# Decoder trunk on one core: the scheduler plans table loads and first landings, the key blocks get column parts of their own, the last products stand behind the gates, and the order is new

## The chip, the core and the metric

The kernel runs on one core of one Trainium2 chip: TensorE (PE) multiplies, VectorE (DVE), ScalarE (ACT) and GpSimd (POOL) do the elementwise work, SyncE (SP) issues the DMAs, and 16 DMA engines carry them. The metric is device microseconds of one execution. A measurement here is a median of three runs.

## The reference

Two layers of a decoder trunk over 256 tokens of width 1024, in float32. Per layer, cut to what matters:

```python
proj = rmsnorm(h, norm_g[i]) @ w_in[i]          # 14 groups of columns
# HGRN2: a gated linear recurrence over 4 heads (q, forget gate f, input, two output gates)
log_f = logaddexp(log(lb), log1p(-lb) + log_sigmoid(fl)); k_hg = (1 - lb) * sigmoid(-fl)
o_hg = hgrn2_chunkwise(q, log_f, k_hg, v)
y_hg = rmsnorm(o_hg) * sigmoid(hgo) * silu(hz)
# NSA: 8 heads, three branches over keys: compressed blocks, selected blocks, window
p_cmp = masked_softmax(q_nope @ kc.T * scale); o_cmp = p_cmp @ vc
o_nsa = gates[0]*o_cmp + gates[1]*selected_attn(q_rope, ...) + gates[2]*window_attn(q_rope, ...)
h = h + concat([y_hg, o_nsa * silu(nz)]) @ w_out[i]
gate = sigmoid(rmsnorm(h, ple_norm_g[i]) @ w_pg[i])
h = h + gate * (p[i] @ w_pp[i])
```

## The kernel before

**Products in three passes.** Every large product splits both operands in a rounded part and a rest (`xh`, `xl` and `hi`, `lo`, in the fp32r format) and sums three matmuls of 128 rows by 256 columns. A chunk of 256 weight columns (1 MB) is 48 such matmuls in one PSUM bank. There are three banks for this (`mm_63`, `mm_64`, `mm_65`), four for all else (`ax`), and one for the attention output (`po`). The `w_in` columns make 17 chunks (`hi0` to `nz1`; the chunk `kk` has 280 columns and takes two banks), and after them come `w_pp`, four chunks of `w_out` and four of `w_pg`.

**Loads and splits.** `loader` issues all weight DMAs from SP, in the order of the list `ORDER`, into four 1 MB buffers (`raw`). `splitter` makes `hi` (L505, on ACT or POOL) and `split_lo` makes `lo` (L511 on DVE, L512 on POOL) of a quarter chunk at a time, in a ring of nine buffers (`hl`). The weights `w1` of the compression go through the same `raw` buffers and hold two of them until their product (L986).

**What follows a chunk.** The chunks `hf` give the gates F and K (ACT Sigmoid), `hi` gives the values `tV` (L740, scaled by a factor that the row norm delivers), `hq` the queries. `tree` builds the decayed products of the recurrence: `near` for steps inside 32 tokens (L776), `blocks(32)` and `blocks(64)` for the larger ones (L835, evacuated by ACT, L839), then a last scaling of `tQ` and `tK` (L396 on DVE, L397 on POOL) and the product of `hgrn` (L888). `cmp_softmax` runs beside it: an Exp on ACT (L1291), a mask, sums. `attention` makes eight units per layer of scores, Exp, transposes and products (L1384 to L1442, L1360). `pp` multiplies p by `w_pp` (L1553) and keeps the result; `ev_pg` takes a `w_pg` bank, scales it (L1623), makes the gate with a Tanh, multiplies by the kept product and adds to h. The last `w_pg` chunk goes out in two halves (`ev_tail`, `tail_part`, L1662 to L1669).

**What sets the order.** `Sched.run` plays all of this at build time as threads of operations on planned clocks of five engines. At each step it takes the operation with the smallest planned start plus a weight (`WGT`) times a priority (`PRI`); some operations may go to one of two or three engines by a bias (`PREF`). The order it finds is the program's order on each engine. Its costs are plain numbers (`dS`, `dV`, `dG`); a change of ScalarE's function table has none. One table load stands at the start (L385); the others stand where a function first needs one:

```python
    S.activation(warm, ones, AF.Sigmoid)
    for _ in range(7):
        PE.matmul(sch.pools["ax"][-1].ap, lhsT=zb, rhs=zb[:, None, :].to_broadcast([128, 4, 128]),
```

Each engine takes its instructions strictly in this order, so an operation that waits holds all that stand behind it.

## Time and profile before

| | us |
|---|---|
| median of 3 runs (lowest to highest) | 392.29 (390.48 to 392.95) |
| the profiled execution, its own time | 392.22 |
| its span, first to last instruction | 390.4 |
| PE busy in the span | 379.2 |
| DVE, ACT, POOL busy | 309.3, 263.4, 126.2 |

A start time in a row counts from the start of the span. "Idle before" names the engine's idle time ahead of an instruction and what ended it. A busy time of PE is the time in which at least one matmul was in flight; matmuls overlap, so the pace is read from one start to the next. PEclk is the granted TensorE clock: 1.00 is the level of 2.4 GHz and 0.50 that of 1.2 GHz.

### The profile page before, as it was taken

What the parts mean: (1) busy time and instruction counts of PE and PEld (TensorE: products, weight loads), DVE (VectorE), ACT (ScalarE), POOL (GpSimd) and SP (SyncE); (2) the same over time, 40 slices, a digit from 0 to 9 for tenths busy, and PEclk for the clock granted to TensorE, in tenths of its full rate; (3) what the DMA queues carried; (4) which work ended last, traced back from release to release, by engine and by line L of the source; (5) the groups of instructions that cost most, each with busy time, mean ns of one, the idle gap of its engine ahead of it and who ended that gap; (6) DMA issues with size and microseconds to landing.
All of it is one profiled execution on the core that took longest, in us unless ns stands there. A gap on an engine that the chain in (4) does not pass through costs nothing.

```text
span 390.4 us, 9546 instructions
## 1 busy us (share of the span) xinstructions
PE 379.2 (97%) x3681; PEld 365.3 (94%) x3681; DVE 309.3 (79%) x731; ACT 263.4 (67%) x611; POOL 126.2 (32%) x195
## 2 busy tenths in 40 slices
PE   8989999999999999999999999999989999999995
PEld 4979999999899999999998999999989999999994
DVE  4984789999779875598978769999978787748864
ACT  6964455467788987486765945645878897857621
POOL 3000554556237544000000035724733755400100
PEclk9999999999999999999999999999999999999999
DMA  7995556454224431346446355935434342233011
GB/s 250 405 421 203 187 219 250 138 190 166 97 90 156 169 109 49 133 146 217 164 170 215 121 206 163 375 112 175 152 107 138 109 169 68 91 109 107 2 54 55
DMA packets 12285, 63.02 MB, mean 161 GB/s; under 512 B 1616, under 2 KB 2768, under 8 KB 5584
## 3 DMA queue, kind: packets, MB, share of 16 engines
q1 hardware_dynamic: 12240, 62.42, 44.5%
q8 instruction: 29, 0.48, 0.5%
q14 instruction: 16, 0.13, 0.1%
HBM read 61.36 MB, written 1.05 MB: 160 GB/s over the span
## 4 chain that ended last, share of the span: by engine, by line
PE 84%; DVE 6%; ACT 3%; DMA 3%; issue 1%; SPq 1%; DVEq 0%; ACTq 0%
PE mm L549 65%; DMA raw<-w_in 3%; PE po L1360 3%; PE mm L1553 3%; PE ax L1435 3%; DVE lo L511 2%; PE ax L776 2%; PE ax L1384 1%; ACT hi L505 1%; PE ax L1385 1%; PE ax L986 1%; SPq L400 1%; PE ax L1127 1%; PE po L1346 1%; ACT L1291 1%
## 5 line engine op out<-in xcount | busy, mean ns | idle before, releaser
L505 ACT ACTIVATE hi<-raw 128x512 fp32r<-128x512 f32 (+2 forms) x209 | 129.5, 628 | 83.0 <-PE mm L549 71.9
L549 PE MATMUL mm<-xh,hi 128*128 128x256 f32 x608 | 176.4, 290 | 1.8 <-ACT tV L740 1.8
L511 DVE TENSOR_TENSOR lo<-raw,hi 128x512 fp32r<-128x512 f32 (+2 forms) x201 | 142.1, 718 | 38.5 <-ACT hi L505 33.0
L549 PE MATMUL mm<-xl,hi 128*128 128x256 f32 x608 | 171.5, 282 | 0.0
L549 PE MATMUL mm<-xh,lo 128*128 128x256 f32 x608 | 171.1, 281 | 0.0
L549 PEld LDWEIGHTS mm<-xh,hi 128*128 128x128 f32 x608 | 115.1, 189 | 4.3 <-ACT tV L740 2.0
L549 PEld LDWEIGHTS mm<-xh,lo 128*128 128x128 f32 x608 | 115.7, 190 | 0.2 <-DVE lo L511 0.2
L549 PEld LDWEIGHTS mm<-xl,hi 128*128 128x128 f32 x608 | 115.4, 190 | 0.3
L549 PE MATMUL mm<-hi,xh 128*128 128x256 f32 (+1 forms) x192 | 55.5, 289 | 1.0 <-DVE t L1623 0.8
L549 PE MATMUL mm<-lo,xh 128*128 128x256 f32 (+1 forms) x192 | 54.5, 284 | 0.6 <-DVE lo L511 0.5
L549 PE MATMUL mm<-hi,xl 128*128 128x256 f32 (+1 forms) x192 | 54.1, 282 | 0.0
L1418 POOL TENSOR_SCALAR P<-P,s 128x128 f32<-128x128 f32 (+1 forms) x64 | 41.9, 673 | 30.4 <-DVE s L1411 12.3
L549 PEld LDWEIGHTS mm<-hi,xh 128*128 128x128 f32 x192 | 36.1, 188 | 2.6 <-ACT hi L505 1.4
L549 PEld LDWEIGHTS mm<-lo,xh 128*128 128x128 f32 x192 | 36.1, 188 | 1.2 <-DVE lo L511 1.2
L598 POOL TENSOR_TENSOR s<-s,mhalf 128x2 f32<-128x2 f32 x4 | 3.4, 846 | 104.1 <-DVE s L594 104.1
L549 PEld LDWEIGHTS mm<-hi,xl 128*128 128x128 f32 x192 | 36.2, 188 | 0.0
L1398 ACT ACTIVATE P<-P,s 128x128 f32<-128x128 f32 (+1 forms) x64 | 28.3, 447 | 0.0
L1393 DVE CUSTOM_DVE_ANT_0 P<-ax,cn 128x128 f32<-128x128 f32 (+1 forms) x64 | 20.3, 352 | 7.3 <-PE ax L1385 4.6
L1191 POOL TENSOR_TENSOR s<-s,mhalf 128x4 f32<-128x4 f32 x4 | 4.6, 1151 | 42.2 <-DVE s L1187 42.2
L397 POOL TENSOR_TENSOR md<-t,rp 128x32 f32<-128x32 f32 (+1 forms) x32 | 14.7, 479 | 6.3 <-DVE t L1111 4.0
L1442 ACT ACTIVATE PT<-ax 128x512 f32<-128x512 f32 x24 | 14.2, 592 | 3.1 <-PE ax L1435 3.1
L1435 PE MATMUL ax<-cn,P 128*128 128x128 f32 x96 | 14.5, 273 | 0.0
(210 smaller groups left out, 579.5 us busy)
## 6 DMA issues: line engine op xcount, KB each, us to landing
raw<-w_in SPq DMA_DIRECT2D x28, 1024.0 KB, 5.0
raw<-w_out SPq DMA_DIRECT2D x8, 1024.0 KB, 4.9
raw<-w_pg SPq DMA_DIRECT2D x8, 1024.0 KB, 4.8
raw<-w SPq DMA_DIRECT2D x4, 1024.0 KB, 5.0
...
raw<-w_pp SPq DMA_DIRECT2D x2, 1024.0 KB, 4.8
...
```

Source lines behind the costliest of these rows:

```text
L397: ("G", dG2(n), lambda: G.tensor_tensor(out, in0, in1, op=fn), PREF["t2_G"])], r, w)
L505: ("S", dS(m), lambda: S.activation(hi, src, AF.Copy), 0.0)], rt, ht_)
L511: yield alt([("V", dV2(m), lambda: V.tensor_tensor(lo, src, hv, op=OP.subtract), 0.0), ("G", dG2(m), lambda: G.tensor_tensor(lo, src, hv, ...
L549: PE.matmul(out, lhsT=a, rhs=b, start=k == 0 and i == 0 and (j == 0 or nb == 2), stop=k == NK - 1 and i == 2, skip_group_check=True)
L776: PE.matmul(pa[r0:r0 + 32, g], lhsT=Kx[:, hd, b:b + 32], rhs=qx[:, :, hd, b:b + 32], start=True, stop=True)
L1360: PE.matmul(po.ap[64 * par:64 * par + 64, tt * 128:(tt + 1) * 128], lhsT=vn[:, st, b, par], rhs=PTs[tt][par][b * (tt + 1) + st], start=Fal ...
L1393: yield op("V", dV(ns) + 0.02, lambda: V.tensor_tensor_reduce(P[:, b], sv[:, b], cn[:, CN_CA + 128 - ns + 128:CN_CA + 256], -1.0, 3.0e38, ...
L1398: yield op("S", dS(ns, 2), lambda: S.activation(P[:, b], P[:, b], AF.Exp, bias=nm.ap[:, b:b + 1], scale=-1.0, accum_out=sm_.ap[:, b:b + 1] ...
L1418: ("G", dG(ns) + 0.05, lambda: G.tensor_scalar(P[:, b], P[:, b], w, 1.0, op0=OP.mult, op1=OP.mult), PREF["P_G"]),
L1435: PE.transpose(tb.ap[:, i * 128:(i + 1) * 128], Ps[par][1][:, b, st * 128:(st + 1) * 128], idf)
L1442: ("S", dS(w_), lambda: S.activation(PT.ap[:, 0:w_], tb.ap[:, 0:w_], AF.Copy), PREF["PT_S"])],
L1553: PE.matmul(bk.ap[:, j * 256:(j + 1) * 256], lhsT=x[:, k, w], rhs=y[:, t], start=k == 0 and i == 0, stop=k == 1 and i == 2)
```

## The change

- **Order searched anew.** `ORDER` starts with `hf0, hi1, hi0` and ends with `nz0`; all planner tables (`WGT`, `PREF`, `MARG`, `STAY`, `PRI`) have new numbers. The compression weights `w1` are loaded after the fifth chunk and no longer after the ninth.
- **Table loads are planned.** An ACT operation may name its table; a change of table costs the planner 1.28, and a new thread issues a one-element Exp once all Sigmoids of a layer are done, and a one-element Sigmoid once the attention of the first layer is.
- **First landings.** The first two pieces of the first chunk are issued from ACT's queue, the first table load stands behind them, and the planner counts 1.0 and 0.6 more for two landings of h. The first two chunks may take their `hi` on DVE.
- **Column parts.** In `blocks`, key blocks of the two token halves write different partitions of PSUM, so that neighbouring matmuls use different columns of the array: two parts of 64, or four of 32. Each half gets its own evacuation on ACT. The compressed keys are repeated to 120 columns.
- **Last products.** p is halved when it is split. In the last layer the fourth `w_pp` chunk is multiplied after the last `w_pg` matmul; the gates are made meanwhile, and the sum reads the product from PSUM. The halves of 128 tokens are gone.

```diff
-ORDER = ["hi0", "hf0", "hi1", "hq0", "kk", "cm", "hf1", "hq1", "nq0", "hgo0", "nq1", "vv", "hz0", "nz0", "hz1",
-         "hgo1", "nz1"]
+ORDER = ["hf0", "hi1", "hi0", "hq0", "kk", "cm", "hf1", "hq1", "nq0", "hgo0", "nq1", "vv", "hz0", "hz1", "nz1",
+         "hgo1", "nz0"]
-BUFS = dict(mm=3, ax=4, raw=4, w1=8, t5=3, P=4, PT=5, t2=2, au=3, hl=9, wt=9)
+BUFS = dict(mm=3, ax=4, raw=4, w1=4, t5=3, P=4, PT=5, t2=2, au=3, hl=9, wt=9)
...
+            if isinstance(dur, Act) and dur.table != self.table:
+                end, self.table = end + 1.28, dur.table
+                self.eng[eng] = end
...
-    S.activation(warm, ones, AF.Sigmoid)
...
+        if act:
+            return op("S", Load(0.43, kb), lambda: nc.scalar.dma_start(out=out, in_=src), w=w)
...
-        pa, pb = pieces(items[0], (1, 1, 2, 2, 2)), pieces(items[1], (2, 2, 2, 2))
+        pa, pb = pieces(items[0], (1, 1, 2, 2, 2), 2), pieces(items[1], (2, 2, 2, 2))
         yield from next(pa)
+        yield from next(pa)
+        yield op("S", 1.49, lambda: S.activation(warm, ones, AF.Sigmoid))
...
+                if key in (items[0][0], items[1][0]):
+                    ch.append(("V", dVf(m), lambda: V.tensor_copy(hi, src), PREF["hi_V"]))
...
-                pa = bk.ap.rearrange("p (g t) -> p g t", g=8)
+                pa = bk.ap[:, 0:4 * lv].rearrange("p (h t) -> p h t", h=4)
+                bs = [(b % 128 // (2 * lv) * 2 * lv + b // 128 * lv, b) for b in range(0, T, 2 * lv)]
...
-                        for b in range(0, T, 2 * lv):
-                            r0 = b % 128
-                            PE.matmul(pa[r0:r0 + lv, 2 * hd + b // 128, 0:lv], lhsT=K[:, hd, b:b + lv],
+                        for r0, b in bs:
+                            PE.matmul(pa[r0:r0 + lv, hd], lhsT=K[:, hd, b:b + lv],
                                       rhs=Q[:, hd, b + lv:b + 2 * lv], start=True, stop=True)
...
-                for b in range(0, 128, 2 * lv):
-                    yield op("S", dS(8 * lv), lambda: S.activation(
-                        AT[b:b + lv, :, b + lv:b + 2 * lv], pa[b:b + lv, :, 0:lv], AF.Copy), bk.t + [att], [att])
+                for r0, b in bs:
+                    c, d0 = b // 128, b % 128
+                    yield op("S", dS(4 * lv), lambda: S.activation(
+                        AT[d0:d0 + lv, c::2, d0 + lv:d0 + 2 * lv], pa[r0:r0 + lv], AF.Copy), bk.t + [att], [att])
...
+        def table(fn, name, evs):
+
+            for ev in evs:
+                yield wait(ev)
+            yield op("S", Act(name, 0.2), lambda: S.activation(warm, ones, fn))
...
+        def pp_last(hb, px):
+
+            yield wait(e("zlast"))
+            for j in range(2):
+                bk = yield alloc("mm")
+                yield pp_mm(hb, px, j, bk, bk.ap[:, 0:T])
+                sch.spawn(out_last(bk, j), PRI["pg"])
...
+        def out_last(bk, j):
+            u = yield wait(e("gate", j))
+            hv = h[:, 6 + j]
+            yield op("V", dV(T), lambda: V.scalar_tensor_tensor(u.ap, u.ap, 1.0, bk.ap[:, 0:T], op0=OP.add,
+                                                                op1=OP.mult), bk.t + u.t, u.t)
+            bk.free()
+            yield op("V", dV2(T), lambda: V.tensor_tensor(hv, hv, u.ap, op=OP.add), u.t + [ht[6 + j]], [ht[6 + j]])
```

What the new order is shows at three places. The first is ACT in layer 0, at the splits of the chunk `kk` (the rows with 560 elements; `tV` from `mm_63` and `mm_65` is the evacuation of `hi0` and `hi1`). Before:

```order
L505 ACTIVATE hi_91<-raw_96 128x560
L505 ACTIVATE hi_93<-raw_96 128x560
L505 ACTIVATE hi_77<-raw_96 128x560
L505 ACTIVATE hi_79<-raw_96 128x560
L740 ACTIVATE tV_102<-mm_63,s_140 128x256 x2
L609 ACTIVATE R_129<-ax_67 128x256
L505 ACTIVATE hi_81<-raw_97 128x512
L740 ACTIVATE tV_102<-mm_65,s_140 128x256 x2
```

Now, with `hi1` in `mm_64` and `hi0` in `mm_65`:

```order
L534 ACTIVATE hi_91<-raw_96 128x560
L774 ACTIVATE tV_102<-mm_64,s_140 128x256 x2
L534 ACTIVATE hi_93<-raw_96 128x560
L774 ACTIVATE tV_102<-mm_65,s_140 128x256 x2
L641 ACTIVATE R_129<-ax_67 128x256
L534 ACTIVATE hi_77<-raw_96 128x560
L534 ACTIVATE hi_79<-raw_96 128x560
```

The evacuation of the bank that the next chunk takes (`mm_63` before, `mm_64` now) moves from behind four splits of `kk` to behind one. The second place is PE at the border of the two layers: the last matmuls of layer 0's fourth `w_pg` chunk (with `xh_71`, `xl_72`) and the first of layer 1 behind them (with `xh_73`, `xl_74`). Before:

```order
L549 MATMUL mm_64<-xh_71,hi_79 128x256
L549 MATMUL mm_64<-xl_72,hi_79 128x256
L549 MATMUL mm_64<-xh_71,lo_80 128x256
L549 MATMUL mm_64<-hi_85,xh_73 128x256
L549 MATMUL mm_64<-lo_86,xh_73 128x256
```

Now (the six matmuls into `mm_64` and the six into `mm_63` are cut to their first):

```order
L581 MATMUL mm_65<-xh_71,hi_79 128x256
L581 MATMUL mm_65<-xl_72,hi_79 128x256
L581 MATMUL mm_65<-xh_71,lo_80 128x256
L581 MATMUL mm_64<-xh_73,hi_87 128x256
...
L581 MATMUL mm_63<-hi_89,xh_73 128x256
...
L581 MATMUL mm_65<-hi_91,xh_73 128x256
```

Twelve matmuls of layer 1 that were open in the other two banks now stand between the last `w_pg` matmul and the first one that takes its bank again. The third place is ACT in layer 0, late in the tree, around the Exp of `cmp_softmax` (`at<-ax_67` is the evacuation of `blocks(64)`). Before:

```order
L1153 ACTIVATE tq_0_111<-ax_68,h 64x2x256 x2
L1291 ACT_TABLE_LOAD
L1291 ACTIVATE md_136<-md_136 128x240
L505 ACTIVATE hi_91<-raw_96 128x512
L1462 ACTIVATE t_0_114<-t_1_115 128x512
L839 ACTIVATE at<-ax_67 64x8x64
```

Now:

```order
L1189 ACTIVATE tq_0_111<-ax_69,h 64x2x256 x2
L1504 ACTIVATE t_0_114<-t_2_116 128x512
L534 ACTIVATE hi_89<-raw_96 128x512
L875 ACTIVATE at<-ax_67 64x4x64
L1333 ACTIVATE md_137<-md_137 128x240
L875 ACTIVATE at<-ax_67 64x4x64
```

The table load is gone from here (it stands some forty rows earlier, behind the second pair of Sigmoids), and the Exp stands between the two halves of the evacuation. Counted over the whole program, PE has as many instructions as before; 18 of 191 `lo` of 512 elements went from DVE to POOL, 60 small rope operations from POOL to DVE, and ACT still loads a table four times.

## Rows read from the trace of the kernel before

**Rows 1.** The profile's page: the busy time of the engines (share of the span, instructions), and the share of each engine in the chain of work that ended last.

```profile
PE 379.2 (97%) x3681; PEld 365.3 (94%) x3681; DVE 309.3 (79%) x731; ACT 263.4 (67%) x611; POOL 126.2 (32%) x195
PE 84%; DVE 6%; ACT 3%; DMA 3%; issue 1%; SPq 1%; DVEq 0%; ACTq 0%
```

**Rows 2.** Pieces of the chain of work that ended last: start, length, what, and the number of instructions merged in it.

```profile
15.85 7.21 DMA raw<-w_in
...
64.72 1.03 PE ax L776 x64
...
93.59 0.50 PE ax L835 x32
...
97.78 0.97 PE ax L835 x14
...
132.29 1.46 PE po L1360 x24
...
159.17 20.69 PE mm L549 x174
```

**Rows 3.** The waits of PE over the whole run: who waited for whom, us in total, times, longest.

```profile
PE ax L888 <- DVE tQ L396: 1.9, 2, 1.0
PE mm L549 <- ACT tV L740: 1.8, 1, 1.8
```

**Rows 4.** The timeline at the border of the layers, on PE and DVE.

```profile
206.02 0.28 PE L549 MATMUL mm<-xh,lo 128*128 128x256 f32 x1
...
206.34 0.69 DVE L1623 TENSOR_TENSOR t<-mm,R 128x512 f32<-128x512 f32 x1 [0.17 <-PE mm L549]
...
207.08 0.39 PE L549 MATMUL mm<-hi,xh 128*128 128x256 f32 x1 [0.78 <-DVE t L1623]
```

**Rows 5.** Stretches behind the longest pause of PE and, last, behind the product of `hgrn` in layer 0: from:to and length, busy us (instructions) of PE, weight loads, DVE, ACT and POOL, then the granted clock of TensorE, the DMA engines' busy share, and GB/s.

```profile
26.28:32.00 5.72, 5.72 (x35) 5.72 (x36) 3.09 (x6) 3.76 (x8) 0.00 (x0) 0.70 0.91 377
32.00:38.00 6.00, 6.00 (x49) 6.00 (x49) 3.72 (x6) 3.05 (x5) 0.00 (x0) 1.00 0.50 171
102.77:108.00 5.23, 5.17 (x40) 4.73 (x41) 5.10 (x22) 3.45 (x16) 0.09 (x1) 1.00 0.43 138
```

**Rows 6.** A stretch inside the tree of layer 0, columns as in Rows 5.

```profile
70.00:80.00 10.00, 10.00 (x141) 9.78 (x140) 9.89 (x20) 4.84 (x10) 6.46 (x10) 1.00 0.57 206
```

**Rows 7.** The timeline of all engines around the end of the third chunk: start, length, engine, line, operation, and idle before it. The last row of PE before the pause is the one at 24.24.

```profile
22.50 0.82 POOL L598 TENSOR_TENSOR s<-s,mhalf 128x2 f32<-128x2 f32 x1 [18.26 <-DVE s L594]
...
23.14 2.35 ACT L505 ACTIVATE hi<-raw 128x560 fp32r<-128x560 f32 x4 [2.88 <-DMA raw<-w_in]
...
24.24 0.28 PE L549 MATMUL mm<-hi,xl 128*128 128x256 f32 x1
...
24.58 0.16 DVE L657 COPY s<-s 128x2 f32<-128x2 f32 x1
...
25.40 0.82 ACT L740 ACTIVATE tV<-mm,s 128x256 f32<-128x256 f32 x2
...
26.27 0.39 PE L549 MATMUL mm<-xh,hi 128*128 128x256 f32 x1 [1.76 <-ACT tV L740]
```

**Rows 8.** The timeline at the end of the tree: of layer 0 on ACT, DVE and PE, and the PE rows of layer 1.

```profile
98.75 1.28 ACT L1291 ACT_TABLE_LOAD   x1
100.05 0.41 ACT L1291 ACTIVATE md<-md 128x240 f32<-128x240 f32 x1
...
101.60 0.28 PE L549 MATMUL mm<-xh,lo 128*128 128x256 f32 x1
101.70 0.39 DVE L1294 TENSOR_REDUCE s<-md 128x16 f32<-128x240 f32 x1
...
102.21 0.42 DVE L396 TENSOR_TENSOR tQ<-tQ,tot 128x256 f32<-128x256 f32 x1
...
102.77 0.91 PE L888 MATMUL ax<-tQ,tK 128*128 128x128 f32 x6 [0.90 <-DVE tQ L396]
...
289.85 0.28 PE L549 MATMUL mm<-xh,lo 128*128 128x256 f32 x1
291.13 1.13 PE L888 MATMUL ax<-tQ,tK 128*128 128x128 f32 x8 [1.00 <-DVE tQ L396]
```

**Rows 9.** The evacuation of the blocks on ACT, over the whole run: least, median and largest duration in ns, first and last start, forms.

```profile
L839 ACT ACTIVATE at<-ax x6: 377/378/592, 94.1 to 289.9; 32x256 f32<-32x256 f32 x4, 64x512 f32<-64x512 f32 x2
```

**Rows 10.** The timeline of the end, on PE and DVE.

```profile
385.39 0.28 PE L549 MATMUL mm<-xh,lo 128*128 128x256 f32 x1
385.70 0.49 DVE L1662 TENSOR_TENSOR t<-mm,R 128x128 f32<-128x128 f32 x2 [1.01 <-PE mm L549]
...
387.22 0.29 DVE L1669 TENSOR_TENSOR h<-h,t 128x128 f32<-128x128 f32 x1
```

**Rows 11.** Groups of instructions by line and form: line, engine, operation, count, busy us, mean ns of one, and idle before.

```profile
L511 DVE TENSOR_TENSOR lo<-raw,hi 128x512 fp32r<-128x512 f32 x191 | 135.6, 720 | 37.2 <-ACT hi L505 31.8 <-PE ax L1435 2.6 <-PE ax L934 0.9
...
L512 POOL TENSOR_TENSOR lo<-raw,hi 128x512 fp32r<-128x512 f32 x8 | 11.0, 1380 | 7.7 <-ACT hi L505 5.0 <-DVE md L1285 2.7
L397 POOL TENSOR_TENSOR md<-t,rp 128x64 f32<-128x64 f32 x16 | 9.0, 584 | 4.0 <-DVE t L1111 4.0
```

**Rows 12.** The weight loads on the page's list of DMA issues: count, KB each, median us from issue to landing.

```profile
raw<-w_in SPq DMA_DIRECT2D x28, 1024.0 KB, 5.0
```

**Rows 13.** The timeline at the product of the compression weights in layer 0.

```profile
51.79 1.48 PE L986 MATMUL ax<-raw,PT 128*32 128x128 f32 x46
```

More of the change, by code (lines that the diff above doesn't have):

```diff
@@ L118, in __new__ @@
         return x
+class Load(float):
+    def __new__(cls, dur, kb):
+        x = float.__new__(cls, dur)
+        x.kb = kb
+        return x
+class Act(float):
+    def __new__(cls, table, dur):
+        x = float.__new__(cls, dur)
+        x.table = table
+        return x
 class Thread:
@@ L133, in __init__ @@
         self.kind = "r"
+        self.table = "sigmoid"
         self.pools = {}
@@ L226, in run @@
                 self.port["V"] = end
+            if isinstance(dur, Act) and dur.table != self.table:
+                end, self.table = end + 1.28, dur.table
+                self.eng[eng] = end
+            if isinstance(dur, Load):
+                self.landed = max(self.landed, end + 1.7) + dur.kb / 405.0
+                end, eng = self.landed, "D"
             for x in th.req[2]:
@@ L443, in loader @@
                 b = yield alloc("raw")
-                yield dma(b.ap[:, 0:2048], it[1], 1024, b.t, 2.0)
+                yield dma(b.ap[:, 0:2048], it[1], 1024, b.t)
                 sch.e(*it[0]).set(b)
@@ L458, in loader, with pieces @@
                 sch.e("masks").set()
-    def pieces(it, ns):
+    def pieces(it, ns, na=0):
         key, src, n = it
@@ L1022, in mm2 @@
                 def mm2():
-                    PE.matmul(pk[0:32, 0:64], lhsT=hv.ap[:, 120:152], rhs=w2.ap[:, 0:64], start=True,
-                              stop=True)
+                    PE.matmul(pk[0:120, 0:64], lhsT=hk, rhs=w2.ap[:, 0:64], start=True, stop=True)
                     PE.matmul(pk[0:120, 64:128], lhsT=hv.ap[:, 0:120], rhs=w2.ap[:, 64:128], start=True,
                               stop=True)
-                yield op("P", Mat("c", 0.36), mm2, hv.t + w2.t, kb.t)
+                yield op("P", Mat("t", 0.36), mm2, hv.t + w2.t, kb.t)
                 w2.free()
@@ L1363, in pair @@
                 bufs = list(dict.fromkeys(x.buf for tt in ts for x in PTs[tt]))
-                yield op("P", Mat("c", sum(0.53 * (tt + 1) - 0.02 for tt in ts)), mm,
+                yield op("P", Mat("c", sum(0.49 * (tt + 1) - 0.05 for tt in ts)), mm,
                          [t for x in bufs for t in x.t] + Vn.t, po.t)
@@ L1544, in pp @@
                 hb = yield wait(sch.e("hl", (l, "pp"), c))
-                hi, lo = (x[:, 0:512].rearrange("p (k n) -> p k n", k=2) for x in hb.ap)
+                if l == L - 1 and c == 3:
+                    sch.spawn(pp_last(hb, px), PRI["w_pg"] + 4)
+                    break
                 bk = yield alloc("mm")
                 for j in range(2):
-                    def mm():
-                        w = slice(j * 128, (j + 1) * 128)
-                        for k in range(2):
-                            t = slice(k * T, (k + 1) * T)
-                            for i, (x, y) in enumerate(((hi, ph), (hi, pl), (lo, ph))):
-                                PE.matmul(bk.ap[:, j * 256:(j + 1) * 256], lhsT=x[:, k, w], rhs=y[:, t],
-                                          start=k == 0 and i == 0, stop=k == 1 and i == 2)
-                    yield op("P", 0.707, mm, hb.t + px.t, bk.t)
+                    yield pp_mm(hb, px, j, bk, bk.ap[:, j * 256:(j + 1) * 256])
                 hb.free()
@@ L1558, in pp, with pp_mm, mm @@
                 yield op("S", dS(512), lambda: S.activation(
-                    dst.ap[:, 512 * (c % 2):512 * (c % 2) + 512], bk.ap, AF.Copy, scale=0.5), bk.t,
+                    dst.ap[:, 512 * (c % 2):512 * (c % 2) + 512], bk.ap, AF.Copy), bk.t,
                     dst.t[2 * (c % 2):2 * (c % 2) + 2])
                 bk.free()
-            px.free()
-            e("PP").set((A, B))
+            if l < L - 1:
+                px.free()
+            e("PP").set((A, B))
+        def pp_mm(hb, px, j, bk, out):
+            hi, lo = (x[:, 0:512].rearrange("p (k n) -> p k n", k=2) for x in hb.ap)
+            ph, pl = px.ap
+            def mm():
+                w = slice(j * 128, (j + 1) * 128)
+                for k in range(2):
+                    t = slice(k * T, (k + 1) * T)
+                    for i, (x, y) in enumerate(((hi, ph), (hi, pl), (lo, ph))):
+                        PE.matmul(out, lhsT=x[:, k, w], rhs=y[:, t], start=k == 0 and i == 0,
+                                  stop=k == 1 and i == 2)
+            return op("P", 0.707, mm, hb.t + px.t, bk.t)
+        def pp_last(hb, px):
[4 more added lines that the diff above has]
+                sch.spawn(out_last(bk, j), PRI["pg"])
+            hb.free()
+            px.free()
+        def out_last(bk, j):
[5 more added lines that the diff above has]
+            yield op("V", dV2(T), lambda: V.tensor_tensor(hv, hv, u.ap, op=OP.add), u.t + [ht[6 + j]], [ht[6 + j]])
+            u.free()
+            yield dma(d["yT"][:, 6 + j], hv, 128, [ht[6 + j]])
         def ev_out(c):
@@ L1704, in layer @@
         sch.spawn(cmp_softmax(), PRI["csm"])
+        sch.spawn(table(AF.Exp, "exp", [e("FK"), e("FK", 0), e("FK", 1)]), PRI["tab"])
+        if l + 1 < L:
+            sch.spawn(table(AF.Sigmoid, "sigmoid", [e("PT", i, t) for i in range(4) for t in range(2)]), PRI["tab"])
         sch.spawn(attention(), 9)
```

102 lines of the change are left out of this document (45 added, 57 removed).

## The prediction

> **What bounds the kernel now.** I read the share of busy time first, then the chain of work that ended last, then the waits of PE, and last the timeline at each of these waits. PE has a matmul in flight for 379.2 us, and the chain is 84% PE [rows 1]: what ends the run late is PE's own work and the few places where PE stands. On the product path 174 matmuls take 20.69 us, 0.119 us each [rows 2]; "lost" below is the time from start to start beyond this pace. The waits name the two heavy places, tQ at the tree ends (1.9 us in all) and tV in the third chunk (1.8) [rows 3]; a third is the 0.78 idle at the border of the layers [rows 4]. One loss stands in no list of waits: after the longest pause PE is busy all the time, but at a granted clock of 0.70 on average [rows 5]. DVE is nearly full in the tree (9.89 of 10 us) [rows 6], so it is the engine that could take over. I work against the profiled execution, 392.22, which lies 0.07 below the median; 1.8 of it is outside the span, and I leave that as it is.
>
> **1. The pause at 24.2.** The last matmul starts at 24.24 and the next at 26.27: 2.03, less 0.12, is 1.91 lost [rows 7]. The released thing is the bank of the chunk `hi0`: ACT evacuates it at 25.40 in 0.82, and ahead of this stand four splits of `kk` (2.35, or 0.59 each), which start when `kk` has landed, at 15.85 + 7.21 = 23.06 [rows 2, 7]. Now one split stands ahead, and the bank to be reused is the first one evacuated: 23.14 + 0.59 + 0.82 = 24.55, and PE resumes about 24.6. The evacuation also needs the scale factor. Its power is made on POOL by 22.50 + 0.82 = 23.32, and the DVE copy (0.16) that came at 24.58 now stands ahead of the `lo` of `kk`, so the factor is there by 23.6 [rows 7]. Next late is this landing itself: if `kk` lands later, the whole moves with it. PE then stands 0.2 to 0.4 instead of 1.91. Gain 1.5 (bounds: 0 if the landing slips by that much, 1.9 if PE does not stand).
>
> **2. The clock behind it.** From 26.28 to 32.00 the granted clock is 0.70 on average, and from 32.00 on 1.00 [rows 5]. Of 5.72 us, 0.30 x 5.72 = 1.7 are lost; the count of instructions agrees (35 in 5.72 us, against 49 in 6.00 in the next stretch). It fell after PE had stood 1.91 us; behind the stop of 1.05 (part 4) the clock stayed at 1.00 [rows 5]. Matmuls that are back within 0.4 us should keep level 1.00. Gain 1.7, or 0: there is no row between.
>
> **3. The border of the layers.** From 206.02 to 207.08, 0.94 is lost, while DVE takes 0.69 to empty the bank [rows 4]. Twelve open matmuls, 12 x 0.119 = 1.43, now stand in the gap and cover 0.31 + 0.69 + hand-off. Gain 0.94. They are work of layer 1 that only moves. What needs the sixth and seventh slices of h comes 54 matmuls (6.4 us) into the layer, behind a chain of some 4.5 us of gate, sum and split (an estimate from one 0.69 and about nine steps of 0.4).
>
> **4. The tree ends.** 101.60 to 102.77 loses 1.05, 289.85 to 291.13 loses 1.16 [rows 8]. What is late is the last scaling of `tQ` at 102.21, behind a reduction (101.70) on DVE that needs the Exp of `cmp_softmax` (100.05), which waited for a table load of 1.28 at 98.75 [rows 8]. The load stands some forty ACT rows earlier now, where ACT has slack (busy 4.84 of the 10 us from 70 on) [rows 6], and the evacuations follow at once. Between the product of `blocks(64)` and that of `hgrn` stand 36 matmuls instead of 24, so 4.3 us of cover, while evacuations, one scaling each of `tQ` and `tK` on DVE (0.42 each) and hand-offs come to about 2.9. Gain 2.1 of 2.21 (down to 0, or a loss: rival C).
>
> **5. Column parts.** `blocks(32)` takes 0.50 for 32 matmul rows, 16 ns each, in two parts of 32 columns; `blocks(64)` 0.97 for 14 rows, 69 ns each, in one part; `near` with four parts has 16 ns for 64 moving columns, and the 128 moving columns of the attention output with two parts of 64 take 1.46/24 = 61 ns [rows 2]. So the time goes as moving columns over parts. Two parts of 64 halve 0.97: 0.49. Four parts for `blocks(32)` would give 8 ns a row, and no row here is that short: between 0 and 0.25, I take 0.12. Per layer 0.6, together 1.2 (bounds 0 to 1.5; 0 if parts that share a bank don't run together, which the rows of `near` speak against). The evacuations double in number and halve in width. They were 0.38 (256 wide) and 0.59 (512) [rows 9]; at 128 and 256 wide I take 0.28 and 0.38, so per layer 4 x 0.28 + 2 x 0.38 = 1.88 instead of 1.35: 0.5 more on ACT, inside the cover of part 4. If that cover were gone, it would cost 1.0.
>
> The Trainium skill, page "TensorEngine Tiling (Array Packing)", section "PSUM Bottleneck", speaks against this part: tiling makes the matmuls quicker and not the evacuation, so that the copy out of PSUM may become the limit. By that rule the 1.2 won would be given back but for 0.2; by the rows, where ACT has the slack named in part 4, it is kept, and I weigh the rule in rival C.
>
> **6. The tail.** Before, h is done at 387.22 + 0.29 = 387.51, 2.12 after the last matmul's start at 385.39 [rows 10]. Now the matmuls of `w_pp` come last (same count, moved), and the gates, whose scaling and Tanh took 0.49 and 0.51 in their two halves, are made beside the 12 matmuls (1.43). Behind the last one: 0.31 to DVE's start, one product and one sum of 256 columns (0.42 each by the row of `tQ`) and 0.04 between: 1.19 [rows 8, 10]. Gain 0.93. If the gates come late, it is down to 0.4.
>
> **Costed at nothing.** The start: the first matmul waits for the warm-up matmuls, so issuing the first pieces from ACT brings nothing by itself, and PE stands at `kk` anyway, behind what six `hi` on DVE may cost (0.3 to 0.7 each). The table loads stay four. Halving p and widening the compressed keys to 120 columns replace operations one for one. 18 `lo` go from DVE (720 ns) to POOL (1380 ns), together 13.0 us off DVE [rows 11]. 60 small rope operations go the other way: on DVE 0.16 (the copy of two elements) to 0.29 (128 columns) each, 10 to 17 us; on POOL they took up to 584 ns [rows 7, 10, 11]. So DVE's load stays, and each moved `lo` arrives 0.66 later, covered by the chunks that are split ahead of PE. Its price without cover is rival D. PE has as many instructions as before.
>
> **Sum.** 1.5 + 1.7 + 0.94 + 2.1 + 1.2 + 0.93 = 8.4; 392.2 - 8.4 = **383.8**.
>
> **Rivals.**
> **A, the sum holds** (382.8 to 385.5; low: every term at its upper bound, 9.4; high: parts 5 and 6 bring 0.5 instead of 2.1), 0.50.
> **B, the early pause stays long enough to drop the clock.** `kk` lands late as before: 7.21 against the median of 5.0 [rows 2, 12]. The order of the DMAs ahead of it has changed, which may make it earlier or later. Without term 2 alone 385.5, without 1 and 2 387.0; 0.13.
> **C, the tree ends wait as before.** DVE, full there, carries the rope operations and the scaling of `tK` as well, and the doubled evacuations stand behind splits. Without term 4, 385.9; with another microsecond at each end 387.9. For it: [rows 6]; against it: the third more cover. 0.12. The page's rule named in part 5 ends here too, at 384.8 with its 1.0 given back, inside A.
> **D, new waits eat the gain.** The order is another one throughout. 18 late `lo` of 0.66 are up to 11.9 us of delay; if half reaches PE, 383.8 + 6.0 = 389.8. For it: DVE's and POOL's `lo` are waited for by every chunk, and POOL is slower; against it: PE's waits for `lo` are so small before that none is in the list's first two. From half on it comes within 1% of before. 0.15.
> **E, slower than before.** The compression weights come after the fifth chunk and hold two of the four `raw` buffers until their product, at 51.79 before [rows 13]. Until then four chunks share the other two: a buffer turns in a landing plus some 2.5 us of splitting (2.35 on ACT) [rows 7], while PE spends 2 x 48 x 0.119 = 11.4 us on two chunks. It decides from a landing of about 8.8 us on; the median is 5.0 and the one on the chain 7.21 [rows 2, 12]. At landings of 11.5, four turns are each 2.6 us late: 383.8 + 10.4 = 394.2. Slower by over 1% (above 396.2) needs landings of 12.0 at least. 0.07, and I give it whole to slower.
> **F, below 382.8**, by holes too short for the lists: 0.03.
>
> **How the numbers follow.** Within about 1% (388.4 to 396.2) a measurement of this kernel can't well tell a change from none. A, B, C and F lie below 388.4: faster 0.78. D holds 0.15 about the bound, same; E 0.07, slower. The range goes from 382.0 (F's near half) to 389.8 (D at its worked value): about half of D and all of E are left out, 0.15 to 0.2. A alone is 382.8 to 385.5.
>
> **What would show it.** Right: the evacuation of the bank that the fourth chunk takes at about 23.7, PE back by 24.6, and a granted clock of 1.00 from 26 to 32; no idle before the first PE row of layer 1 into the reused bank; no wait of the `hgrn` product for `tQ`, and the load of the Exp table ahead of `blocks`; `blocks(64)` about 0.5 and `blocks(32)` 0.25 to 0.5; 1.2 from the last matmul to the last sum. Wrong: clock 0.50 early on (B), `hgrn` after a wait for `tQ`, `tK` or `at` (C), PE's waits for `lo` from POOL above 2 us in all (D), waits for `raw` or `hi` between 25 and 52 (E). The sum fails as a whole if PE's pace of 0.119 is lost in stretches that I have not looked into, by the new order of its products.

## The result and the profile after

The changed kernel takes 386.94 us (median of 4 runs, 386.33 to 387.23) against 391.63 (4 runs, 390.48 to 392.95): ratio 0.9877, 95% interval 0.9839 to 0.9915. Measured once more beside later experiments it took 386.56 (6 runs, 386.06 to 388.65), ratio 0.9890 (0.9865 to 0.9914). So it is 1.1 to 1.2% faster, inside the range and 3.1 us above the likeliest value. The profiled execution took 386.33, its span is 384.4.

The page of the changed kernel, busy time and shares of the chain, and the waits of PE (who waited for whom, us in all, times, longest):

```profile
PE 375.0 (98%) x3681; PEld 362.6 (94%) x3681; DVE 310.5 (81%) x791; ACT 260.6 (68%) x611; POOL 114.0 (30%) x135
PE 75%; DVE 15%; DMA 5%; issue 2%; ACT 1%; POOL 0%; SPq 0%; POOLq 0%; ACTq 0%; DVEq 0%
```

```profile
PE ax L1426 <- DVE tPCl L1357: 1.4, 2, 0.7
PE ax L1253 <- POOL t L1246: 1.2, 1, 1.2
...
PE ax L1022 <- DVE PT L420: 0.7, 1, 0.7
PE ax L1037 <- ACT t L1028: 0.5, 1, 0.5
```

Neither wait of [rows 3] is left in PE's list, and four others stand there. DVE's share of the chain rose from 6% to 15% [rows 1]: the run now waits for DVE more than before, though DVE is as busy as it was.

The places that the prediction named, in the changed kernel. Its timeline at the end of the third chunk and the stretch behind it (columns as in [rows 5]):

```profile
22.35 0.67 ACT L534 ACTIVATE hi<-raw 128x560 fp32r<-128x560 f32 x1 [2.67 <-DMA raw<-w_in]
...
22.93 0.82 ACT L774 ACTIVATE tV<-mm,s 128x256 f32<-128x256 f32 x2
...
23.29 0.38 PE L638 MATMUL ax<-cn,s 128*128 128x128 f32 x2
...
23.80 0.39 PE L581 MATMUL mm<-xh,hi 128*128 128x256 f32 x1
```

```profile
26.28:32.00 5.72, 5.72 (x49) 5.72 (x48) 2.93 (x5) 3.03 (x7) 0.00 (x0) 1.00 0.84 327
```

One split stands ahead of the evacuation, the next matmul follows at 23.80, 0.41 behind the second of the two small ones (L638) ahead of it, and the clock stays at 1.00: 49 matmuls where [rows 5] had 35.

Its timeline at the border of the layers, where DVE empties the bank and PE takes it again:

```profile
199.31 0.69 DVE L1694 TENSOR_TENSOR t<-mm,R 128x512 f32<-128x512 f32 x1 [0.17 <-PE mm L581]
...
200.41 0.28 PE L581 MATMUL mm<-hi,xl 128*128 128x256 f32 x1
...
200.52 0.28 PE L581 MATMUL mm<-hi,xh 128*128 128x256 f32 x1
```

The bank is empty at 200.00, and the matmul that takes it follows at 200.52, 0.11 behind the last of the twelve: nothing is lost.

Its timeline at the tree's end in layer 0:

```profile
97.55 0.39 ACT L1333 ACTIVATE md<-md 128x240 f32<-128x240 f32 x1
...
98.30 0.42 DVE L420 TENSOR_TENSOR tQ<-tQ,tot 128x256 f32<-128x256 f32 x1
...
98.95 0.41 DVE L420 TENSOR_TENSOR tK<-tK,tot 128x256 f32<-128x256 f32 x1
...
99.71 1.06 PE L924 MATMUL ax<-tQ,tK 128*128 128x128 f32 x8
```

The Exp has its table, both scalings are done before the `hgrn` product (L924), and no wait stands in that row, against 0.90 and 1.00 in [rows 8].

Its last matmul and DVE's last product and sum:

```profile
380.17 0.28 PE L1612 MATMUL mm<-pxh,lo 128*128 128x256 f32 x1
...
380.65 0.41 DVE L1629 SCALAR_TENSOR_TENSOR t<-t,mm 128x256 f32<-128x256 f32 x1
...
381.10 0.42 DVE L1632 TENSOR_TENSOR h<-h,t 128x256 f32<-128x256 f32 x1
```

From the last matmul's start to the end of the span it is 384.4 - 380.17 = 4.23; before it was 390.4 - 385.39 = 5.01 [rows 10].

The terms, in the two profiled executions ("lost" as in the prediction, start to start less 0.12):

| | forecast | measured |
|---|---|---|
| 1 pause at 24 | 1.5 | 1.91 - 0.29 = 1.62 |
| 2 clock behind it | 1.7 | 1.7 in this execution, fewer in the median (below) |
| 3 border of the layers | 0.94 | 0.94 |
| 4 tree ends | 2.1 | 2.21 at the place |
| 5 column parts | 1.2 | 1.33 in the matmuls |
| 6 tail | 0.93 | 0.78 |
| start, not forecast | 0 | 0.85 in this execution (the rest of 26.27 - 23.80 = 2.47) |
| new waits | 0 | -4.7 |

The new waits are 0.84 at 48.4 and 0.68 at 52.5 (compression), 0.83 each at 103.7 and 291.0 (third score product), 0.22 at 234.9 and 1.32 at 242.8 (transposes of the keys). The table adds up to 4.7; the executions differ by 392.22 - 386.33 = 5.9, and the remaining 1.2 lies in pieces under half a microsecond, which are not broken down. The terms were there, then, and half of them came back elsewhere.

### The profile page after: what moved, and what is told of

Read it like the earlier page. It is cut to its first block, busy times and chain, and to the rows that moved or that the text cites. A ratio compares the mean times of both kernels' runs of the same rounds, so it can differ in the third digit from the quotient of the medians.

```text
span 384.4 us, 9516 instructions
## 1 busy us (share of the span) xinstructions
PE 375.0 (98%) x3681; PEld 362.6 (94%) x3681; DVE 310.5 (81%) x791; ACT 260.6 (68%) x611; POOL 114.0 (30%) x135
## 4 chain that ended last, share of the span: by engine, by line
PE 75%; DVE 15%; DMA 5%; issue 2%; ACT 1%; POOL 0%; SPq 0%; POOLq 0%; ACTq 0%; DVEq 0%
PE mm L581 58%; DMA raw<-w_in 5%; PE po L1402 3%; PE mm L1612 3%; PE ax L1477 3%; DVE lo L543 3%; DVE PT L420 2%; PE ax L1426 2%; PE ax L810 1%; PE ax L1427 1%; DVE tK L420 1%; DVE tq L1191 1%; DVE tQ L420 1%; DVE t L1499 1%; PE po L1388 1%
## 5 line engine op out<-in xcount | busy, mean ns | idle before, releaser
L534 ACT ACTIVATE hi<-raw 128x512 fp32r<-128x512 f32 (+1 forms) x203 | 123.4, 628 | 51.9 <-PE mm L581 38.3
L543 DVE TENSOR_TENSOR lo<-raw,hi 128x512 fp32r<-128x512 f32 (+2 forms) x183 | 125.7, 704 | 25.0 <-ACT hi L534 24.2
L544 POOL TENSOR_TENSOR lo<-raw,hi 128x512 fp32r<-128x512 f32 x26 | 36.7, 1416 | 57.4 <-ACT hi L534 57.4
L1460 POOL TENSOR_SCALAR P<-P,s 128x128 f32<-128x128 f32 (+1 forms) x64 | 38.6, 618 | 34.3 <-DVE s L1453 18.5
```

Source lines behind the costliest of these rows:

```text
L534: ("S", dS(m), lambda: S.activation(hi, src, AF.Copy), 0.0)]
L543: yield alt([("V", dV2(m), lambda: V.tensor_tensor(lo, src, hv, op=OP.subtract), 0.0), ("G", dG2(m), lambda: G.tensor_tensor(lo, src, hv, ...
L544: ("G", dG2(m), lambda: G.tensor_tensor(lo, src, hv, op=OP.subtract), PREF["lo_G"])],
L1460: ("G", dG(ns) + 0.05, lambda: G.tensor_scalar(P[:, b], P[:, b], w, 1.0, op0=OP.mult, op1=OP.mult), PREF["P_G"]),
```

## The experiments

All play back the changed kernel's order, entry by entry, with only the named entries moved (the diffs show that order) or the named lines changed. Theory 1 says that each new wait has a cause of its own in what stands ahead of an operation or runs beside it; theory 2, that a wait taken away returns as the next one. The first four experiments were measured on one chip and the others on another; the kernel before took 391.11 on the first and 391.66 and 390.86 on the second.

**lo_dve: three `lo` back to DVE** (DVE, layer 0; one more in layer 1):

```diff
 L420 TENSOR_TENSOR PT_122<-tqn_103,h 128x8x15 x4
 L1264 SCALAR_TENSOR_TENSOR tkl_113<-ax_68,h,tkh_112 128x2x128
+L543 TENSOR_TENSOR lo_92<-raw_96,hi_91 128x512
 L1264 SCALAR_TENSOR_TENSOR tkl_113<-ax_68,h,tkh_112 128x2x128
 L717 TENSOR_TENSOR t_1_115<-mm_65,R_129 128x512
+L543 TENSOR_TENSOR lo_94<-raw_96,hi_93 128x512
```

> The changed kernel with three of its lo (two in layer 0, one in layer 1) taken back from POOL to DVE, behind the eight two-input DVE operations that make the operand of the compression product; nothing else moves. In the changed kernel three of these DVE operations took 1.33 to 1.37 us instead of 0.34, each beside a POOL lo of 1.3 to 1.4. Theory 1 (the missing part of the forecast gain lies in new waits of PE, each made by what stands ahead in one engine's order or beside it): these operations take 0.34 again, the wait in the middle of the compression product (0.96 at 48.4, 0.34 at 234.9) goes, and the next one (0.80 at 52.5), whose chain starts behind the same DVE operations, shrinks; the run gets 1.0 to 1.7 us shorter than the changed kernel. Theory 2 (each removed wait comes back as the next one, since the splits of the weights set the pace there): under 0.4 us shorter.

384.53 us (383.97 to 385.22), ratio 0.9819 (0.9789 to 0.9849); its span is 1.1 shorter than the changed kernel's (2.0 to 2.4 in the medians). First the changed kernel's timeline at the compression product, on DVE, POOL and PE, then the eight operations by tile (least, median, largest ns, first and last start):

```profile
45.22 4.32 DVE L420 TENSOR_TENSOR PT<-tqn,h 128x120 f32<-128x120 f32 x8
...
45.92 2.69 POOL L544 TENSOR_TENSOR lo<-raw,hi 128x512 fp32r<-128x512 f32 x2 [0.43 <-ACT hi L534]
...
47.56 1.08 PE L1022 MATMUL ax<-raw,PT 128*32 128x128 f32 x32
...
49.33 1.08 PE L1022 MATMUL ax<-raw,PT 128*32 128x128 f32 x32 [0.69 <-DVE PT L420]
```

```profile
L420 DVE TENSOR_TENSOR PT<-tqn,h x8: 339/350/1368, 45.2 to 49.2; 128x120 f32<-128x120 f32 x8
```

And the same eight in this experiment:

```profile
L420 DVE TENSOR_TENSOR PT<-tqn,h x8: 353/358/418, 46.2 to 48.2; 128x120 f32<-128x120 f32 x8
```

Without the two POOL `lo` beside them the eight take 0.35 to 0.42, the group takes 2.3 instead of 4.3, and the wait inside the compression product is gone in both layers; the one at 52.5 shrinks from 0.68 to 0.25. (In layer 0 a wait of 0.60 for a POOL copy appears at 56.1, and the one at 242.8 shrinks from 1.32 to 0.61.) Theory 1 holds here. In the changed kernel's trace the operations of this kind that came to a running POOL `lo` ended only behind it, three of them after 1.33 to 1.37: they stood still while POOL made the `lo`.

**tpc_first: one operation ahead of two** (DVE, both layers):

```diff
 L1517 SCALAR_TENSOR_TENSOR tQ<-t_0_114,t_2_116 128x512
+L1357 TENSOR_TENSOR tPCl<-ax_69,tPCh 120x256
 L1541 SCALAR_TENSOR_TENSOR tQ<-t_1_115,tQ 128x512
 L1499 TENSOR_TENSOR t_0_114<-mm_64,R_129 128x512
-L1357 TENSOR_TENSOR tPCl<-ax_69,tPCh 120x256
```

> The changed kernel with one DVE operation per layer (tPCl, the rest of the compressed probabilities) moved ahead of two other DVE operations of 0.69, as soon as ScalarE has made tPCh. In the changed kernel the third score product waits for it 0.95 from start to start in each layer, 0.83 beyond the pace. Theory 1: both waits go, 1.5 to 1.7 us shorter. Theory 2: the score product then waits for something else of the same time, or the product bank that the two delayed operations free comes late: under 0.4 us shorter.

385.83 us (385.29 to 386.09), ratio 0.9849 (0.9820 to 0.9879); span 0.6 shorter. The changed kernel's timeline at the place:

```profile
102.62 0.39 ACT L1356 ACTIVATE tPCh<-ax 120x256 fp32r<-120x256 f32 x1 [1.22 <-PE ax L1351]
...
102.99 0.69 DVE L1541 SCALAR_TENSOR_TENSOR tQ<-t,tQ 128x512 f32<-128x512 f32 x1
103.60 0.68 DVE L1499 TENSOR_TENSOR t<-mm,R 128x512 f32<-128x512 f32 x1
...
104.20 0.41 DVE L1357 TENSOR_TENSOR tPCl<-ax,tPCh 120x256 fp32r<-120x256 f32 x1
...
104.67 0.39 PE L1426 MATMUL ax<-tkh,tq 128*128 128x256 f32 x1 [0.67 <-DVE tPCl L1357]
```

tPCl could start at 103.01, when tPCh is made, and stands behind 1.37 of other work. Moved ahead, the product follows 4.12 behind the `hgrn` product instead of 4.96 (both layers), but from there to the first product of P and V it takes 0.56 and 0.51 longer than before. So the truth lies between the theories: the wait goes, and some 0.3 of its 0.83 per layer is won.

**tr_late: the transposes behind 12 more matmuls** (PE, layer 1; of the 12 only the first and the last are shown):

```diff
-L1253 MATMUL ax_68<-cn,t_1_115 128x128 x4
 L581 MATMUL mm_64<-xh_73,hi_91 128x256
...
 L581 MATMUL mm_63<-hi_87,xl_74 128x256
+L1253 MATMUL ax_68<-cn,t_1_115 128x128 x4
```

> The changed kernel with the four transposes of the keys of the second token half of layer 1 moved behind 12 more matmuls (1.43 us). In the changed kernel they wait 1.44 (1.32 beyond the pace) for a POOL copy that took 1.76 beside two DVE lo, where the other three of its kind took 0.62 to 0.9. Theory 1: the wait goes, 1.2 to 1.4 us shorter. Theory 2: the 12 matmuls need lo or banks that are not there earlier, or what needs the keys is late in turn: under 0.4 us shorter.

385.43 us (384.52 to 385.70), ratio 0.9837 (0.9801 to 0.9872). In the changed kernel, on DVE, POOL and PE:

```profile
242.40 1.28 DVE L543 TENSOR_TENSOR lo<-raw,hi 128x512 fp32r<-128x512 f32 x2
242.41 1.76 POOL L1246 TENSOR_SCALAR t<-t 128x512 f32<-128x512 f32 x1 [1.03 <-PE ax L1061]
...
244.22 0.44 PE L1253 MATMUL ax<-cn,t 128*128 128x128 f32 x2 [1.16 <-POOL t L1246]
```

The POOL copy lasts until both `lo` are done and about 0.5 more. (The releaser L1061 named in its row cannot be it, since the copy needs nothing of that product; its input is a rope operation that DVE ended at 242.22.) The wait is gone in the experiment and nothing takes its place: from the start of the compression product to the blocks of layer 1 there are 42.4 us instead of 43.8, 1.4 less, the whole wait. Theory 1. The edit takes away PE's wait and not the slow copy, which still takes 1.75; that the two `lo` make it slow is read from the traces. At 56.14 in the changed kernel the same copy starts ahead of DVE's `lo`: there the copy takes 0.62, and the `lo` 1.03 instead of 0.68.

**all_fix: the three together.**

> The three edits together. Theory 1: the waits are independent and add up, 3.5 to 4.6 us shorter than the changed kernel, about 382.5 to 383.5 us. Theory 2: about 1 us shorter at most, 386.

383.30 us (5 runs, 382.88 to 383.79), ratio 0.9787 (0.9761 to 0.9812); span 381.5, 2.9 shorter than the changed kernel's profiled one, 3.3 to 3.6 in the medians. That is theory 1, near the lower end of its range. The two longest of PE's waits there, behind the start:

```profile
PE ax L1253 <- POOL t L1246: 0.4, 1, 0.4
PE mm L581 <- DVE hi L536: 0.4, 1, 0.4
```

**four_fix: the transposes of layer 0 too**, behind six more matmuls:

```diff
-L1253 MATMUL ax_68<-cn,t_1_115 128x128 x4
 L581 MATMUL mm_64<-xh_71,hi_85 128x256
...
 L581 MATMUL mm_64<-xh_71,lo_86 128x256
+L1253 MATMUL ax_68<-cn,t_1_115 128x128 x4
```

> The kernel with the three edits, and the transposes of the keys of the second token half moved behind six more matmuls in layer 0 as well; there they wait 0.71 for the same kind of POOL copy (1.11 beside two DVE lo). Theory 1 (an independent wait): 0.5 to 0.7 us shorter, about 382.7. Theory 2: under 0.2 us shorter.

382.90 us (5 runs, 382.44 to 383.13), ratio 0.9787 (0.9763 to 0.9811); the span is 381.0. It beats both kernels: 3.7 below the changed kernel (386.56 on the same chip). Against the three edits the span is 0.5 shorter; the intervals don't tell the two apart. The control beside it:

> The changed kernel itself once more, beside the next three on the same chip: 386.3 to 387.3 us if its runs repeat, with a granted clock of 0.998 or more in every one.

It took 386.56, as told above; one of its six runs took 388.65. That one was profiled: four `lo` in a row stood on POOL beside the same DVE operations, and the compression product waited 1.8 instead of 0.7; another 0.6 was lost at the start, of the kind shown under no_early_load. The changed kernel's own runs scatter at this place.

**one_part: both token halves in the same partitions again.**

```diff
-pa = bk.ap[:, 0:4 * lv].rearrange("p (h t) -> p h t", h=4)
-bs = [(b % 128 // (2 * lv) * 2 * lv + b // 128 * lv, b) for b in range(0, T, 2 * lv)]
+pa = bk.ap.rearrange("p (g t) -> p g t", g=8)
+bs = [(b % 128, b) for b in range(0, T, 2 * lv)]
...
-PE.matmul(pa[r0:r0 + lv, hd], lhsT=K[:, hd, b:b + lv],
+PE.matmul(pa[r0:r0 + lv, 2 * hd + b // 128, 0:lv], lhsT=K[:, hd, b:b + lv],
...
-AT[d0:d0 + lv, c::2, d0 + lv:d0 + 2 * lv], pa[r0:r0 + lv], AF.Copy), bk.t + [att], [att])
+AT[d0:d0 + lv, c::2, d0 + lv:d0 + 2 * lv], pa[r0:r0 + lv, c::2, 0:lv], AF.Copy), bk.t + [att], [att])
```

> The changed kernel with the key blocks of both token halves in the same partitions of PSUM again; the order of all operations and the evacuations in halves stay. Theory A (the columns in parts are what shortens the matmuls of the blocks): they take 3.37 us again instead of 2.04, and the run is 1.3 us longer. Theory B (the evacuations bound this place, so the matmul time is hidden): 0.0 to 0.3 us longer. Theory C (the difference came from the new neighbours in PE's order): the matmuls keep 2.04.

386.69 us (386.46 to 387.04), ratio 0.9860 (0.9812 to 0.9907): no longer than the changed kernel. The rows of PE at both blocks with the matmul that follows, first of the changed kernel, then of this one:

```profile
90.65 0.48 PE L870 MATMUL ax<-tQ,tK 128*32 128x32 f32 x32
91.06 0.39 PE L581 MATMUL mm<-xh,hi 128*128 128x256 f32 x1
...
94.76 0.69 PE L870 MATMUL ax<-tQ,tK 128*64 128x64 f32 x16
95.38 0.39 PE L581 MATMUL mm<-xh,hi 128*128 128x256 f32 x1
```

```profile
90.41 0.68 PE L870 MATMUL ax<-tQ,tK 128*32 128x32 f32 x32
91.02 0.39 PE L581 MATMUL mm<-xh,hi 128*128 128x256 f32 x1
...
94.72 1.15 PE L870 MATMUL ax<-tQ,tK 128*64 128x64 f32 x16
95.79 0.39 PE L581 MATMUL mm<-xh,hi 128*128 128x256 f32 x1
```

Start to start, the blocks take 0.41 and 0.62 with the new parts and 0.61 and 1.07 (from 94.72 to 95.79) without, as in the kernel before (0.50 and 0.97 in the chain, which leaves out the step to the next kind of matmul) [rows 2]: 0.66 per layer, so theory C is out. But the third score product starts at 104.42 here and at 104.67 in the changed kernel, and its wait is gone: PE came there 0.66 later and found tPCl made. What the column parts win, the wait for tPCl takes. So theory B is right in its time, and by that wait, not by the evacuations.

**fix_one_part: the same on top of the three edits.**

> The kernel with the three edits together, but with the key blocks in the same partitions again. In the changed kernel this undoing cost nothing measurable, because the score products of both layers wait there until a fixed time of DVE. With that wait taken away, theory A (the column parts' gain was real and was eaten by that wait): 1.2 to 1.4 us longer than the kernel with the three edits. Theory B (the matmuls of the blocks lie beside other work that ends later in any case): 0.3 us longer at most.

386.14 us (6 runs, 384.61 to 387.47), ratio 0.9867 (0.9840 to 0.9893). In its profiled execution the span is 382.9, 1.4 longer than with the three edits, and the blocks are 1.33 longer with no wait behind them: theory A, in the profile. Its median is 2.8 longer (3.2 longer than that of four_fix, on the same chip), and the runs scatter over 2.9 us; where the rest of that comes from was not settled.

**no_early_load: no early Exp** (the Sigmoid ahead of layer 1 stays):

```diff
-            yield op("S", Act(name, 0.2), lambda: S.activation(warm, ones, fn))
+            yield op("S", Act(name, 0.2), lambda: name == "exp" or S.activation(warm, ones, fn))
```

> The changed kernel without the one-element Exp in both layers, so that the table is loaded ahead of the Exp of the compressed softmax, as before; the order of all else stays. Theory A (the earlier load is what freed the tree ends): the Exp is 1.3 us later, the hgrn product waits again, and the run is 2 to 2.5 us longer. Theory B (the 12 more matmuls between the blocks and the hgrn product already cover the load): no or a short wait ahead of the hgrn product (0 to 0.3 each); but the chain from the Exp to the compressed probabilities, for which the third score product already waits, gets longer by up to 1.3 in each layer less what stands idle in it: 0.5 to 2.6 us longer, and the wait stands at the score product.

390.11 us (10 runs, 389.45 to 390.73), ratio 0.9949 (0.9925 to 0.9973), 3.2 to 3.6 longer. Its timeline in layer 0:

```profile
98.88 1.28 ACT L1333 ACT_TABLE_LOAD   x1
100.18 0.40 ACT L1333 ACTIVATE md<-md 128x240 f32<-128x240 f32 x1
...
102.15 1.13 PE L924 MATMUL ax<-tQ,tK 128*128 128x128 f32 x8 [1.07 <-DVE s L1337]
```

The waits ahead of `hgrn` are back, 1.23 lost in layer 0 and 1.21 in layer 1: theory A. The 36 matmuls of cover alone don't do it. The wait for tPCl stays besides (0.96 lost each), because the chain behind the Exp moves with it. These come to 2.7 us, and the run is longer than either theory forecast. In the profiled execution PE also comes 1.0 later to 23 us, where this kernel does not differ. Rows of its matmuls at the start, and, from the kernel before, a stretch with a granted clock of 0.50 (columns as in [rows 5]):

```profile
8.81 0.41 PE L581 MATMUL mm<-hi,xh 128*128 128x256 f32 x1
9.02 0.41 PE L581 MATMUL mm<-lo,xh 128*128 128x256 f32 x1
...
9.54 0.29 PE L581 MATMUL mm<-lo,xh 128*128 128x256 f32 x1
9.66 0.28 PE L581 MATMUL mm<-hi,xl 128*128 128x256 f32 x1
```

```profile
28.00:30.00 2.00, 2.00 (x12) 2.00 (x11) 0.69 (x1) 1.62 (x3) 0.00 (x0) 0.50 1.00 401
```

Until about 9.4 the matmuls start every 0.21 us, from there on every 0.12. In the stretch at 0.50 they start every 0.21 too (28.26, 28.47, 28.68), so the start seems to have run at the lower level, though the clock column reads 1.00 for it. Of the thirteen profiles with this start, five show it until 8.6 to 10.2 us (this one, after_again, tr_late, fix_one_part and border_back) and come 0.64 to 1.34 later to 23 us than the changed kernel's; in the other eight the pace is 0.12 from about 5.5 on. So this much scatter is in every comparison of two spans, which is why the places above are compared from start to start as well.

**border_back: the cover at the border taken away** (PE; of each six matmuls only the first is shown):

```diff
 L581 MATMUL mm_65<-xh_71,lo_80 128x256
+L581 MATMUL mm_65<-hi_91,xh_73 128x256
...
 L581 MATMUL mm_64<-xh_73,hi_87 128x256
...
 L581 MATMUL mm_63<-hi_89,xl_74 128x256
-L581 MATMUL mm_65<-hi_91,xh_73 128x256
```

> The changed kernel with the 12 matmuls of layer 1 that stand between the last w_pg matmul of layer 0 and the reuse of its bank moved behind the first six into that bank. Theory A (they were the cover of the bank's evacuation): PE waits 0.9 to 1.0 for it, and the run is 0.9 us longer. Theory B (something else now frees the bank in time, or what follows was waiting anyway): 0.3 us longer at most.

387.79 us (387.58 to 388.21), ratio 0.9888 (0.9841 to 0.9936), 0.9 to 1.2 longer: theory A. The wait of before is back, in PE's timeline:

```profile
200.96 0.36 PE L581 MATMUL mm<-hi,xh 128*128 128x256 f32 x1 [0.88 <-DVE t L1694]
```

**pause_back: ACT's old order at `kk`.**

```diff
 L534 ACTIVATE hi_91<-raw_96 128x560
+L534 ACTIVATE hi_93<-raw_96 128x560
+L534 ACTIVATE hi_77<-raw_96 128x560
+L534 ACTIVATE hi_79<-raw_96 128x560
 L774 ACTIVATE tV_102<-mm_64,s_140 128x256 x2
```

> The changed kernel with ScalarE's order at the chunk kk set back alone: the evacuation that frees the fourth chunk's bank stands behind all four splits of kk again and not behind one. Three more splits of 0.63 to 0.67 put it off by 1.9 us, so PE pauses about 2.3 us instead of 0.41. Theory A (a pause of this length is what lowered the granted clock): a stretch at 0.50 of some 3.4 us comes back behind the pause, and the run is 1.9 + 1.7 = 3.6 us longer than the changed kernel. Theory B (the low clock of before had another cause, such as the order of the first chunks or the DMA load there): the clock stays at 1.00, and the run is 1.9 us longer. The pause of 1.44 us late in the changed kernel was not followed by a lower clock.

388.30 us (9 runs, 387.56 to 390.16), ratio 0.9917 (0.9887 to 0.9947). PE stood 1.79 from start to start, and the profiled execution kept its clock:

```profile
25.30:32.00 6.70, 6.70 (x56) 6.70 (x57) 2.81 (x5) 4.36 (x10) 0.00 (x0) 1.00 0.81 312
```

But each run has a mean granted clock over its span, and a fall like that of [rows 5] takes 1.7 of some 390 us, 0.004, from it. (It does not say where in the run the clock fell; only a profile does.) Here two of nine have 0.996 or less, and take 389.69 and 390.16; the other seven have 0.998 or more, median 387.82. Of 44 runs of the kernel before, made beside the experiments, 17 have 0.995 or less and a median of 392.70, the other 27 (one of them at 0.996) a median of 390.78. Of 56 runs of the changed kernel and all those experiments that leave its order at `kk` alone, none has less than 0.997.

**pause_long: PE stands longer**; of the four splits the third and fourth are made twice:

```diff
-L534 ACTIVATE hi_77<-raw_96 128x560
-L534 ACTIVATE hi_79<-raw_96 128x560
+L534 ACTIVATE hi_77<-raw_96 128x560 x2
+L534 ACTIVATE hi_79<-raw_96 128x560 x2
```

> The kernel with ScalarE's old order at the chunk kk, and two of the four splits of kk made twice on ScalarE (the same values written again), so that PE stands 1.3 us longer: about 3.1 us in place of 1.79. Theory A (the longer PE stands there, the likelier the granted clock falls behind it): the clock falls in most of the runs (mean clock of a run 0.996 or less, about 2 us more than the others), against 2 of 9 at 1.79. Theory B (the fall has nothing to do with how long PE stands): the clock falls as seldom as before, and all runs are 1.3 us longer than with the old order alone, about 389.5.

391.09 us (12 runs, 389.36 to 392.06), ratio 0.9979 (0.9957 to 1.0002). PE stood 3.82 from start to start. Stretches behind it:

```profile
27.00:32.00 5.00, 4.41 (x24) 4.41 (x25) 1.99 (x3) 4.24 (x10) 0.00 (x0) 0.66 0.50 172
32.00:38.00 6.00, 6.00 (x51) 6.00 (x51) 2.93 (x5) 2.58 (x5) 0.00 (x0) 1.00 0.40 156
```

Eight of twelve runs have 0.996 or less, median 391.23; the other four 389.48. None of 56 with a pause of 0.7 at most there in the profiles, 2 of 9 at 1.79, 8 of 12 at 3.82: the counts go the way of theory A. They are small: if the ten falls in 21 runs were dealt out by chance, eight or more would land on these twelve about once in 18. The fall costs 1.8 to 2.1 us when it comes, and it does not come every time.

## Why the prediction was right, and where it was off

The forecast "faster" is right, and the six terms came at their places by the mechanisms named, but the sum did not hold: 386.94 lies outside rival A (382.8 to 385.5), which had 0.50. It is inside the range because the range reaches beyond A to the worked value of D, and what filled that room was not D's mechanism. None of the signs of being wrong that the prediction lists appeared. That the range held is in part luck.

- **Terms 1, 3 and 6** came out as worked out, by the mechanism named; border_back shows the cover of term 3 by itself. The tail won 0.78, not 0.93: DVE starts 0.48 behind the last matmul's start, not 0.31.
- **Term 2** has the right cause and the right size, but was counted as certain. The profiled execution of before was one of those in which the clock falls. Over the 44 runs it costs 17/44 x 1.9 = 0.7 on the mean. About 1 us of the forecast was never in the median (392.22 against 391.17 over the 44).
- **Term 4** was right at its place, and the early load was what did it (no_early_load), not the cover. The step that failed is that it looked no further than `hgrn`: the chain of the same Exp goes on through sums and a transpose to tPCl, for which the third score product waits. PE, freed earlier, stood there 0.83 per layer.
- **Term 5** was nearly exact in the matmuls (1.33 for 1.2): 32 columns in four parts go faster than any row of before, 0.41 for 32. In the changed kernel it is worth nothing, since the same wait takes it back (one_part), and it is worth 1.3 as soon as that wait is away (profile of fix_one_part). The twelve evacuations take 0.27 and 0.38 each, and no wait of PE for `at` stands in any list: what the Trainium skill's page in part 5 says may happen did not happen here.
- **"Costed at nothing"** is the step that failed most. It priced the 18 `lo` on POOL by their own lateness (0.66 each), and PE waits for `lo` only 0.2 in all. The cost was beside them: while POOL makes a `lo`, DVE's two-input operations stand (1.37 for 0.34), and while DVE makes two `lo`, a POOL copy stands (1.76 where the kernel before took 0.62). That made the waits at 48.4, 52.5, 234.9 and 242.8, 3.1 us in all. Three of DVE's operations that stood are of the eight per layer that make the compression's operand; DVE and POOL shared those before, four each, and the prediction's count of what moves to DVE leaves them out. The trace agrees with the Trainium skill, "SBUF — State Buffer", section "SBUF: two separate sides", by which a DVE operation with two inputs in SBUF and a GpSimd operation that reads SBUF hold one pair of ports in turn, for a whole instruction each.
- **The rivals.** Of D the amount happened (4.7 of new waits) and not the mechanism. A's lower end is added up wrong: the upper bounds of the six terms come to 9.2 and not 9.4, which gives 383.0. C named the right stretch, but `hgrn` waits no more. B was out for the profiled run. Of E nothing is seen: no wait for `raw` or `hi` stands among PE's between 25 and 52.
- **The start** was costed at nothing. PE starts 0.45 later (DVE's first `hi` takes 0.70), and its last matmul ahead of the pause still starts 0.85 earlier (23.39 against 24.24), since the four holes of before behind the first matmul are smaller. Which part of the edit does that was not tried, and five profiles with the same start come 0.64 to 1.34 later to this place (no_early_load), so one execution does not show that the gain is steady.
